# A two-layer hybrid trunk on one core: the opening with one load queue, a split one-pass norm weight, Pool's low parts and earlier squares

## Chip, cores and metric

The kernel runs on one core of a Trainium2 chip. The metric is device microseconds of one execution. All times in this document are microseconds unless marked otherwise.

## What is computed

The reference runs two layers over x, which is 256 tokens by 1024 features in float32. Each layer has a token mixer and a channel mixer, each of them between two RMS norms:

```python
for l in range(DEPTH):
    h = rms_norm(x, ln_mix_pre[l])
    x = x + rms_norm(hybrid_mixer(h, ...), ln_mix_post[l])
    h = rms_norm(x, ln_ffn_pre[l])
    x = x + rms_norm(conv_ffn(h, ...), ln_ffn_post[l])
```

The mixer projects h by one matrix w_in whose columns feed three head groups: MoBA attention with a relative bias from a table (rel_bias), latent attention with a low-rank query and key/value (each with an RMS norm of its own, q_norm and kv_norm, here called the norms of the latents), and forgetting attention. Their outputs are mixed by w_o. The channel mixer is a GeGLU network with a causal convolution of width 3.

## The kernel before

The two token tiles of 128 rows stand with tokens on partitions (`xt[0]`, `xt[1]`). A product is done in float32r, at one pass each, with both operands split into a high part (rounded to float32r) and a low part (what is left): three products, high·high, high·low and low·high, take the place of one of full precision.

Weights come in slabs of up to 128x1024 float32. The list of slabs is written down once, in order of use (`plan`): for the first layer four slabs "c" (latents, 128x832), four "v" (128x768), then qa0 and qa1 (128x1024), uq, uk, and so on. A slab is loaded into one of five staging buffers (`fetch`, line 195). Its high part is then rounded on ScalarE (`hi_next`, line 207) and its low part subtracted on VectorE (`lo_next`, line 214); the second of these frees the staging buffer, and the next slab's load can be issued. `slab` runs six slabs ahead of use, unless `hold` is set. High and low parts have eight buffers.

Each engine works through its own instructions in the order in which the program issues them. SyncE issues most loads, ScalarE and Pool (GpSimd) a few. In the opening of the first layer this order is written by hand:

- The prenorm of a tile (`prenorm`, line 287) takes two squares with accumulated sums on ScalarE (line 270), three small Pool steps that make the inverse root (lines 275 to 277), and two scalings on VectorE (line 291). They multiply x by the root and by the norm weight, which for the first layer stands in two PSUM banks: it has been spread over the partitions by products of a matrix `ones` with `g0`, whose first row is the weight (line 134).
- `to_feat` transposes a tile on TensorE (line 298) and splits it: high part on ScalarE (line 254), low part on VectorE (line 255). They go to `xh` and `xl`.
- `c_piece(t, h)` multiplies tile t by slab "c" h (lines 248, 249, 251), `v_piece` by slab "v" h. After the "c" pieces, `c_norm` does the norms of the latents: square on ScalarE (line 405), root on Pool (259, 260), scaling on VectorE (407), four times in turn. `c_feat` transposes their result (line 415) behind the "v" pieces, and then come the products with qa0, qa1 and the rest.
- The bias table is built by a small product (`bias_start`, line 329), copied to `rr`, written to memory (`sd`, line 334) and gathered back from there as `hk`, 128x6x256 (line 338), through Pool's queue. It is used much later, in `bias_end` (line 344).

In ScalarE's order the high parts of qa0 and qa1 stand ahead of the squares of the norms of the latents, in both kernels.

Of the kernel before, what the change touches and what calls it, by code (L numbers as in the profile page):

```python
# [10 lines left out]
F32 = mybir.dt.float32  # L11
F32R = mybir.dt.float32r
AF = mybir.ActivationFunctionType
ALU = mybir.AluOpType
AX = mybir.AxisListType

D = 1024
# [16 lines left out]
C_U, C_M, C_R = 0, 128, 384  # L34
# [30 lines left out]
def kernel(ctx: ExitStack, tc: tile.TileContext, x, rel_bias, ln_mix_pre, ln_mix_post,  # L65
                             ln_ffn_pre, ln_ffn_post, w_in, b_f, q_norm, kv_norm, w_uq, w_ukv, w_o,
                             w_up, conv_w, conv_b, w_down, cst_d, oh_d, out):
    nc = tc.nc
# [6 lines left out]
    lay = pool("lay", 1)  # L75
    work = pool("work", 2)
# [7 lines left out]
    def acc():  # L84
        return [wk(), wk()]
# [7 lines left out]
    def tok(t):  # L93
        return slice(t * 128, t * 128 + 128)
# [11 lines left out]


    ctx.enter_context(tc.manual_schedule())
    g0 = work.tile([128, D], F32, name="g0", tag="scr", bufs=2)
    nc.gpsimd.memset(g0, 0.0)  # L110
    oh = work.tile([32, 256 + HA], F32, name="oh", tag="pr", bufs=4)
    for c in (slice(0, 512), slice(512, 1024)):
        nc.sync.dma_start(xt[0][:, c], x_v[0][:, c])
    nc.scalar.dma_start(ident, cst_d[:, 0:128])
    nc.scalar.dma_start(g0[0:1, :], ln_mix_pre[0:1])
    ones = work.tile([128, 128], F32, name="ones", tag="pr", bufs=4)
    nc.vector.memset(ones, 0.0)
    nc.vector.memset(ones[0:1, :], 1.0)
    warm = t2([128, 512])
    nc.vector.memset(warm, 0.0)  # L120
    mhalf = const.tile([128, 1], F32, name="mhalf")
    nc.vector.memset(mhalf, -0.5)
    epsb = const.tile([128, 1], F32, name="epsb")
# [5 lines left out]
    mask = cst[:, C_M:C_M + 256]  # L129
    wps = wk()  # L130
    nc.tensor.matmul(wps, ones, warm, start=True, stop=True)
    gps0 = acc()
    for i in range(2):
        nc.tensor.matmul(gps0[i], ones, g0[:, 512 * i:512 * i + 512], start=True, stop=True)


    def plan():
# [70 lines left out]
        lows.append((h, lo, st, n))  # L208
        loaded[key] = (shaped(h, shp), shaped(lo, shp))

    def lo_next():
        if lows:
            h, lo, st, n = lows.pop(0)
            nc.vector.tensor_tensor(lo[:, :n], st[:, :n], h[:, :n].bitcast(F32), op=ALU.subtract)  # L214

    def split_next():
        hi_next()
        lo_next()
# [23 lines left out]
        nc.tensor.matmul(o, stat[0], mov[1], start=False, stop=False)  # L242
        nc.tensor.matmul(o, stat[1], mov[0], start=False, stop=stop)  # L243

    def mm3s(o, pairs, start, stop):
        n = len(pairs)
        for i, (stat, mov) in enumerate(pairs):
            nc.tensor.matmul(o, stat[0], mov[0], start=start and i == 0, stop=False)  # L248
            nc.tensor.matmul(o, stat[0], mov[1], start=False, stop=False)  # L249
        for i, (stat, mov) in enumerate(pairs):  # L250
            nc.tensor.matmul(o, stat[1], mov[0], start=False, stop=stop and i == n - 1)  # L251
# [13 lines left out]
    def rstd2(src, then=None):  # L265
        junk = work.tile([128, 512], mybir.dt.bfloat16, name="junk", bufs=1)
        ms = small.tile([128, 2], F32, name="ms")
        r = small.tile([128, 2], F32, name="r")
        for i in range(2):
            nc.scalar.activation(junk, src[i], AF.Square, scale=1.0 / 32, accum_out=ms[:, i:i + 1])  # L270
            if i == 0 and then is not None:
                then()

        def fin():
            nc.gpsimd.tensor_tensor(r[:, 0:1], ms[:, 0:1], epsb, op=ALU.add)
            nc.gpsimd.tensor_tensor(r[:, 1:2], r[:, 0:1], ms[:, 1:2], op=ALU.add)
            nc.gpsimd.tensor_tensor(r[:, 0:1], r[:, 1:2], mhalf, op=ALU.pow)
            return r[:, 0:1]
        return fin
# [1 line left out]
    def scr():  # L281
        return work.tile([128, D], F32, name="scr", bufs=2)

    def prenorm(t, g, then=None, mid=None):
        fin = rstd2([xt[t][:, c] for c in HALF], then)
        if mid is not None:
            mid()
        r = fin()
        hn = scr()
        for i in range(2):  # L290
            nc.vector.scalar_tensor_tensor(hn[:, HALF[i]], xt[t][:, HALF[i]], r, g[i], op0=ALU.mult, op1=ALU.mult)
        return hn

    def to_feat(t, hn, xh, xl):
        for q in range(2):
            ps = wk().rearrange("p (c f) -> p c f", c=4)
            for c in range(4):
                nc.tensor.transpose(ps[:, c, :], hn[:, (4 * q + c) * 128:(4 * q + c + 1) * 128], ident)  # L298
            s = (slice(None), slice(4 * q, 4 * q + 4), tok(t))
            split(ps, xh[s], xl[s])  # L300

# [17 lines left out]
    wbias = const.tile([128, HA, S], F32, name="wbias")  # L319

    hk = []

    def bias_loads():
        nc.gpsimd.dma_start(oh[:, :256], oh_d)
        nc.gpsimd.dma_start(oh[:, 256:], rel_bias)

    def bias_start():
        ps = wk()
# [25 lines left out]
    for l in range(L):  # L354
# [16 lines left out]
        def feat(i):  # L371
            return qs[i // 4][:, i % 4, :]

        def nat_piece(ps, nm, t, n, h):
            wh, wl = slab((l, nm, h))
            mm3s(ps[:, :n], [((xh[:, 2 * h + k, tok(t)], xl[:, 2 * h + k, tok(t)]), (wh[:, k, :], wl[:, k, :]))
                             for k in range(2)], h == 0, h == 3)

        def nat(nm, t, n):
            ps = wk()  # L380
# [208 lines left out]
        if l == 0:  # L589
            act_set(EXP_SET)  # L590
            fetch(1)
            hn = [prenorm(0, gps0, lambda: [nc.scalar.dma_start(xt[1][:, c], x_v[1][:, c]) for c in HALF]), None]
            fetch(2, nc.scalar)
            split_next()
            fetch(4, nc.scalar)
            to_feat(0, hn[0], xh, xl)
        else:
            hn = hn_next
# [1 line left out]
        vps = [wk(), wk()]  # L600

        def c_piece(t, h):
            nat_piece(cps[t], "c", t, 416, h)

        def v_piece(t, h):
            nat_piece(vps[t], "v", t, 384, h)
# [3 lines left out]

        if l == 0:
            hold[0] = True
            c_piece(0, 0)
            split_next()
            c_piece(0, 1)
            hn[1] = prenorm(1, gps0)
            split_next()
            bias_loads()
            to_feat(1, hn[1], xh, xl)
            small_loads()  # L620
            nc.sync.dma_start(cst[:, C_R:], cst_d[:, 256 + C_R:])
            hold[0] = False
            for t, h in ((1, 0), (1, 1), (0, 2), (1, 2), (0, 3), (1, 3)):
                c_piece(t, h)
            nc.vector.tensor_copy(identr, ident[:6, :6])
            cn = [c_norm(t, cps[t]) for t in range(2)]
            bias_start()
            for h in range(4):
                for t in range(2):
                    v_piece(t, h)  # L630
            nc.sync.dma_start(cst[:, :C_R], cst_d[:, 256:256 + C_R])
            v_end(0)
            v_end(1)
            c_feat(0, cn[0])
            c_feat(1, cn[1])
        else:
            small_loads()
            hold[0] = False
            c_piece(0, 0)
            c_piece(0, 1)  # L640
            c_piece(0, 2)
            c_piece(0, 3)
            cn0 = c_norm(0, cps[0])
            for h in range(3):
                v_piece(0, h)
            to_feat(1, hn[1], xh, xl)
            v_piece(0, 3)
            v_end(0)
            for h in range(4):
                c_piece(1, h)  # L650
            cn1 = c_norm(1, cps[1])
            c_feat(0, cn0)
            for h in range(4):
                v_piece(1, h)
            v_end(1)
            c_feat(1, cn1)
# [306 lines left out]
```

## Time and profile before

| | |
|---|---|
| runs shown | 654.88, 649.19, 650.67; median 650.67 |
| profiled execution, its own time | 651.27 |
| its span in the trace | 649.5 |
| granted TensorE clock, mean | 0.994 |
| TensorE busy | 631.4 us, 97% of the span |
| VectorE, ScalarE, Pool busy | 452.4, 381.2, 31.6 us |
| loaded from memory | 107.78 MB |

The span runs from the first to the last instruction; the execution's own time has 1.8 us around it. Durations come from the one profiled execution. Engines are called PE (TensorE), DVE (VectorE), ACT (ScalarE), POOL and SP; PEld is TensorE's weight load. In a timeline a row starts with its start and duration; "x4" means four instructions merged, and a bracket holds the idle time before them and what ended it. Matmuls are pipelined, so a duration is longer than the distance to the next one.

### The profile page before, as it was taken

The page shows a single profiled execution, that of the slowest core. Times are in us where ns is not written, and L with a number is a line of the kernel's source. Part 1 is how long each engine was busy: PE and PEld are TensorE (multiplying, and loading weights), DVE is VectorE, ACT ScalarE, POOL GpSimd, SP SyncE. Part 2 cuts the span into 40 slices and gives each one's busy share as a digit, 9 for nine tenths or more (in the row PEclk, how much of TensorE's full clock was granted, in tenths as well). Part 3 has the DMA queues.
Part 4 walks back from the last instruction along what each step waited for, and adds up shares of the span by engine and source line. Part 5 has one row for each costly group of instructions (what it writes and reads, how often), then busy time and mean ns, then how long its engine had stood idle before and what let it go on. Part 6 is the DMA issues. An engine that isn't in the chain of part 4 may idle for free.

```text
span 649.5 us, 11307 instructions
## 1 busy us (share of the span) xinstructions
PE 631.4 (97%) x4290; PEld 569.7 (88%) x4290; DVE 452.4 (70%) x891; ACT 381.2 (59%) x729; POOL 31.6 (5%) x74
## 2 busy tenths in 40 slices
PE   7999999999999999999899999999999999999996
PEld 3998987799999999999688988878998999999974
DVE  4674786576878777766676567757587887777663
ACT  4577557656656555545556666566575665555541
POOL 2110000110000000000031000002100000000001
PEclk9999999999999999999899999999999999999998
DMA  7876343356356765553545833334554665556401
GB/s 248 246 246 211 130 161 100 98 169 193 132 173 217 263 224 170 187 181 107 153 126 150 290 131 132 129 98 129 175 170 149 229 227 195 195 195 195 161 2 65
DMA packets 79402, 109.57 MB, mean 169 GB/s; under 512 B 4013, under 2 KB 69267, under 8 KB 79348
## 3 DMA queue, kind: packets, MB, share of 16 engines
q1 hardware_dynamic: 77762, 106.09, 49.8%
q10 hardware_dynamic: 1250, 1.87, 0.8%
q0 software_dynamic: 336, 0.90, 0.4%
q8 instruction: 33, 0.54, 0.3%
q14 instruction: 21, 0.17, 0.1%
HBM read 107.78 MB, written 1.06 MB: 168 GB/s over the span
## 4 chain that ended last, share of the span: by engine, by line
PE 84%; DVE 6%; ACT 3%; DMA 3%; issue 2%; POOL 1%; DVEq 0%; POOLq 0%; ACTq 0%; SPq 0%
PE wk L248 17%; PE wk L249 16%; PE wk L251 16%; PE wk L241 8%; PE wk L242 8%; PE wk L243 8%; DVE wl L214 2%; DMA st<-in_w_in_dram 2%; PE wk L557 2%; PE wk L565 2%; PE wk L524 1%; ACT wh L207 1%; PE wk L522 1%; ACT junk L270 1%; PE wk L298 1%
## 5 line engine op out<-in xcount | busy, mean ns | idle before, releaser
L214 DVE TENSOR_TENSOR wl<-st,wh 128x1024 fp32r<-128x1024 f32 (+3 forms) x200 | 229.4, 1183 | 80.8 <-ACT wh L207 79.8
L207 ACT ACTIVATE wh<-st 128x1024 fp32r<-128x1024 f32 (+3 forms) x200 | 195.8, 1021 | 39.3 <-PE wk L249 13.7
L248 PE MATMUL wk<-xh,wh 128*128 128x256 f32 x768 | 194.3, 285 | 0.1
L249 PE MATMUL wk<-xl,wh 128*128 128x256 f32 x768 | 192.4, 283 | 0.0
L248 PEld LDWEIGHTS wk<-xh,wh 128*128 128x128 f32 x768 | 147.0, 191 | 2.8 <-issue 1.3
L249 PEld LDWEIGHTS wk<-xl,wh 128*128 128x128 f32 x768 | 147.2, 192 | 0.7
L251 PE MATMUL wk<-xh,wl 128*128 128x256 f32 x768 | 123.6, 283 | 0.1
L251 PEld LDWEIGHTS wk<-xh,wl 128*128 128x128 f32 x768 | 105.9, 192 | 0.5 <-DVE wl L214 0.5
L242 PE MATMUL wk<-wl,hp 128*128 128x512 f32 x176 | 70.0, 398 | 2.0 <-DVE wl L214 2.0
L241 PE MATMUL wk<-wh,hp 128*128 128x512 f32 x176 | 69.6, 396 | 0.8 <-ACT wh L207 0.8
L243 PE MATMUL wk<-wh,hp 128*128 128x512 f32 x176 | 69.1, 393 | 0.0
L249 PE MATMUL wk<-wl,xh 128*128 128x256 f32 (+3 forms) x224 | 65.6, 312 | 2.9 <-DVE wl L214 2.9
L248 PE MATMUL wk<-wh,xh 128*128 128x256 f32 (+3 forms) x224 | 66.8, 316 | 1.2 <-ACT xh L254 0.6
L837 ACT ACTIVATE t<-wk,cv 128x256 f32<-128x256 f32 x88 | 43.7, 559 | 40.8 <-PE wk L251 40.7
L845 DVE SCALAR_TENSOR_TENSOR t<-wk,cv,t 128x255 f32<-128x255 f32 x88 | 41.9, 476 | 32.1 <-ACT t L837 32.1
L251 PE MATMUL wk<-wh,xl 128*128 128x256 f32 (+3 forms) x224 | 45.9, 309 | 0.9 <-DVE xl L255 0.9
L249 PEld LDWEIGHTS wk<-wl,xh 128*128 128x128 f32 x224 | 42.6, 190 | 4.7 <-DVE wl L214 4.5
L248 PEld LDWEIGHTS wk<-wh,xh 128*128 128x128 f32 x224 | 42.7, 191 | 3.1 <-ACT wh L207 1.3
L847 DVE SCALAR_TENSOR_TENSOR t<-wk,cv,t 128x254 f32<-128x254 f32 x88 | 42.4, 482 | 3.1
L242 PEld LDWEIGHTS wk<-wl,hp 128*128 128x128 f32 x176 | 33.5, 190 | 10.5 <-DVE wl L214 4.3
L241 PEld LDWEIGHTS wk<-wh,hp 128*128 128x128 f32 x176 | 33.4, 190 | 7.7 <-ACT wh L207 1.2
L243 PEld LDWEIGHTS wk<-wh,hp 128*128 128x128 f32 x176 | 33.5, 190 | 6.9
(149 smaller groups left out, 688.5 us busy)
## 6 DMA issues: line engine op xcount, KB each, us to landing
st<-in_w_up_dram SPq DMA_DIRECT2D x88, 512.0 KB, 4.7
st<-in_w_down_dram SPq DMA_DIRECT2D x44, 512.0 KB, 4.6
st<-in_w_in_dram SPq DMA_DIRECT2D x24, 512.0 KB, 4.8
st<-in_w_o_dram SPq DMA_DIRECT2D x16, 512.0 KB, 3.1
st<-in_w_in_dram SPq DMA_DIRECT2D x8, 390.0 KB, 7.1
st<-in_w_in_dram SPq DMA_DIRECT2D x8, 384.0 KB, 3.1
st<-in_w_in_dram SPq DMA_DIRECT2D x5, 416.0 KB, 3.3
st<-in_w_in_dram ACTq DMA_DIRECT2D x3, 416.0 KB, 6.5
```

The lines of the kernel that those rows point to most:

```text
L207: nc.scalar.activation(h[:, :n], st[:, :n], AF.Copy)
L214: nc.vector.tensor_tensor(lo[:, :n], st[:, :n], h[:, :n].bitcast(F32), op=ALU.subtract)
L241: nc.tensor.matmul(o, stat[0], mov[0], start=start, stop=False)
L242: nc.tensor.matmul(o, stat[0], mov[1], start=False, stop=False)
L243: nc.tensor.matmul(o, stat[1], mov[0], start=False, stop=stop)
L248: nc.tensor.matmul(o, stat[0], mov[0], start=start and i == 0, stop=False)
L249: nc.tensor.matmul(o, stat[0], mov[1], start=False, stop=False)
L251: nc.tensor.matmul(o, stat[1], mov[0], start=False, stop=stop and i == n - 1)
L557: nc.tensor.transpose(pT[:, kb * 128:kb * 128 + 128], pr[:, kb * 128:kb * 128 + 128], ident)
L837: nc.scalar.activation(y[:, g, :], us[a][:, g, :], AF.Identity, scale=cv[:, 88 + cj:89 + cj], bias=cv[:, 132 + cj:133 + cj])
L845: nc.vector.scalar_tensor_tensor(y[:, g, 1:], u[:, g, :S - 1], cv[:, 44 + cj:45 + cj], y[:, g, 1:], op0=ALU.mult, op1=ALU.add)
L847: nc.vector.scalar_tensor_tensor(y[:, g, 2:], u[:, g, :S - 2], cv[:, cj:cj + 1], y[:, g, 2:], op0=ALU.mult, op1=ALU.add)
```

## The change

The change rewrites the opening of the first layer. All big loads go through SyncE's queue in this order: x of tile 0, slab c0, x of tile 1, c1, c2, c3, v0, then the small tables of the norms, then the rest; only the norm weight's row and the identity stay with ScalarE, and the two loads for the bias table go to Pool at the very start. The norm weight is split into a high and a low row and spread by two one-pass products for each half, on full `ones`. The low parts of c0 and c1 are subtracted on Pool. The squares of tile 1 stand ahead of the split of tile 0 on ScalarE. The bias product comes before the transposes of tile 1. The "c" pieces of the first layer are multiplied in another order (`late`): the products that need a slab's low part come last.

```diff
-    g0 = work.tile([128, D], F32, name="g0", tag="scr", bufs=2)
-    nc.gpsimd.memset(g0, 0.0)
+    g0 = work.tile([1, D], F32, name="g0", tag="scr", bufs=2)
+    nc.scalar.dma_start(g0, ln_mix_pre[0:1])
...
+    gh = lay.tile([128, D], F32R, name="gain", bufs=2)
+    gl = lay.tile([128, D], F32R, name="gain", bufs=2)
+    nc.gpsimd.memset(gh.bitcast(F32), 0.0)
+    nc.gpsimd.memset(gl.bitcast(F32), 0.0)
+    nc.gpsimd.dma_start(oh[:, :256], oh_d)
+    nc.gpsimd.dma_start(oh[:, 256:], rel_bias)
...
-    nc.scalar.dma_start(g0[0:1, :], ln_mix_pre[0:1])
...
-    nc.vector.memset(ones, 0.0)
-    nc.vector.memset(ones[0:1, :], 1.0)
+    nc.vector.memset(ones, 1.0)
...
+    oner = work.tile([128, 128], F32R, name="oner", tag="pr", bufs=4)
+    nc.vector.tensor_copy(oner, ones)
...
+    nc.tensor.matmul(wps[:, :256], ones, warm[:, :256], start=True, stop=True)
...
     for i in range(2):
-        nc.tensor.matmul(gps0[i], ones, g0[:, 512 * i:512 * i + 512], start=True, stop=True)
+        c = slice(512 * i, 512 * i + 512)
+        nc.vector.tensor_copy(gh[0:1, c], g0[:, c])
+        nc.vector.tensor_tensor(gl[0:1, c], g0[:, c], gh[0:1, c].bitcast(F32), op=ALU.subtract)
+        nc.tensor.matmul(gps0[i], oner, gh[:, c], start=True, stop=False)
+        nc.tensor.matmul(gps0[i], oner, gl[:, c], start=False, stop=True)
...
-    def lo_next():
+    def lo_next(eng=None):
...
-            nc.vector.tensor_tensor(lo[:, :n], st[:, :n], h[:, :n].bitcast(F32), op=ALU.subtract)
+            (eng or nc.vector).tensor_tensor(lo[:, :n], st[:, :n], h[:, :n].bitcast(F32), op=ALU.subtract)
...
+        if late:
+            for i, (stat, mov) in enumerate(pairs):
+                nc.tensor.matmul(o, stat[0], mov[0], start=start and i == 0, stop=False)
+            for i, (stat, mov) in enumerate(pairs):
+                nc.tensor.matmul(o, stat[1], mov[0], start=False, stop=False)
+            for i, (stat, mov) in enumerate(pairs):
+                nc.tensor.matmul(o, stat[0], mov[1], start=False, stop=stop and i == n - 1)
+            return
...
             fetch(1)
-            hn = [prenorm(0, gps0, lambda: [nc.scalar.dma_start(xt[1][:, c], x_v[1][:, c]) for c in HALF]), None]
-            fetch(2, nc.scalar)
-            split_next()
-            fetch(4, nc.scalar)
+            for c in HALF:
+                nc.sync.dma_start(xt[1][:, c], x_v[1][:, c])
+            fetch()
+            small_loads()
+            nc.sync.dma_start(cst[:, C_R:], cst_d[:, 256 + C_R:])
+            hn = [prenorm(0, gps0), None]
+            hi_next()
+            lo_next(nc.gpsimd)
+            fin1 = rstd2([xt[1][:, c] for c in HALF])
             to_feat(0, hn[0], xh, xl)
...
             hold[0] = True
+            fetch()
+            hn[1] = prenorm(1, gps0, fin=fin1)
             c_piece(0, 0)
-            split_next()
+            hi_next()
+            lo_next(nc.gpsimd)
             c_piece(0, 1)
-            hn[1] = prenorm(1, gps0)
-            split_next()
-            bias_loads()
-            to_feat(1, hn[1], xh, xl)
-            small_loads()
-            nc.sync.dma_start(cst[:, C_R:], cst_d[:, 256 + C_R:])
+            bias_start()
+            to_feat(1, hn[1], xh, xl, hi_next)
+            lo_next()
             hold[0] = False
...
             cn = [c_norm(t, cps[t]) for t in range(2)]
-            bias_start()
```

In VectorE's order before, from the scalings of tile 0 (`scr<-x_84`) on, the low parts of c0, c1 and c2 (`wl`, 128x832) stand between the steps of the two tiles; `xl` is the low part of a transposed tile and `x_85` is tile 1:

```order
L291 SCALAR_TENSOR_TENSOR scr<-x_84,r,wk 128x512 x2
L214 TENSOR_TENSOR wl<-st,wh 128x832
L255 TENSOR_TENSOR xl<-wk,xh 128x4x128 x2
L214 TENSOR_TENSOR wl<-st,wh 128x832
L291 SCALAR_TENSOR_TENSOR scr<-x_85,r,wk 128x512 x2
L214 TENSOR_TENSOR wl<-st,wh 128x832
L255 TENSOR_TENSOR xl<-wk,xh 128x4x128 x2
L214 TENSOR_TENSOR wl<-st,wh 128x832
L214 TENSOR_TENSOR wl<-st,wh 128x768 x4
```

The same place in the changed kernel, where `gain` is the split norm weight and `rr` the bias row:

```order
L144 TENSOR_TENSOR gain<-g_90,gain 1x512
L311 SCALAR_TENSOR_TENSOR scr<-x_84,r,wk 128x512 x2
L275 TENSOR_TENSOR xl<-wk,xh 128x4x128 x2
L311 SCALAR_TENSOR_TENSOR scr<-x_85,r,wk 128x512 x2
L349 MEMSET rr 6x128
L350 COPY rr<-wk 6x256
L275 TENSOR_TENSOR xl<-wk,xh 128x4x128 x2
L226 TENSOR_TENSOR wl<-st,wh 128x832 x2
L226 TENSOR_TENSOR wl<-st,wh 128x768 x4
```

The low parts of c0 and c1 have gone, that of c2 has moved from ahead of tile 1's `xl` to behind it, and the copy of the bias row has come in between.

In Pool's order before, the bias row is written out (`sd`) and gathered (`hk`) behind the four roots of the norms of the latents, of which the last is the first two rows here:

```order
L259 TENSOR_TENSOR r<-ms,epsb 128x1
L260 TENSOR_TENSOR r<-r,mhalf 128x1
L334 DMA sd<-rr 6x384
L336 DMA jm<-in_cst_dram 128x128
L338 DMA hk<-sd 128x6x256
L275 TENSOR_TENSOR r<-ms,epsb 128x1
```

In the changed kernel the same three DMAs follow the second low part, and the roots of the latents (L279) come behind them:

```order
L226 TENSOR_TENSOR wl<-st,wh 128x832
L295 TENSOR_TENSOR r<-ms,epsb 128x1
L296 TENSOR_TENSOR r<-r,ms 128x1
L297 TENSOR_TENSOR r<-r,mhalf 128x1
L226 TENSOR_TENSOR wl<-st,wh 128x832
L352 DMA sd<-rr 6x384
L354 DMA jm<-in_cst_dram 128x128
L356 DMA hk<-sd 128x6x256
L279 TENSOR_TENSOR r<-ms,epsb 128x1
```

The gather has moved past the roots of the latents, and the two low parts stand on either side of tile 1's root.

## Rows read from the trace of the kernel before

**Rows 1.** Stretches: length, busy PE PEld DVE ACT POOL, PEclk, DMA share, GB/s.
```profile
0.00:16.88 16.88, 12.13 (x34) 6.51 (x34) 7.73 (x15) 8.44 (x15) 4.39 (x13) 1.00 0.75 245
16.88:60.00 43.12, 43.03 (x284) 39.40 (x284) 28.56 (x67) 27.92 (x58) 5.62 (x11) 1.00 0.75 241
60.00:130.00 70.00, 69.91 (x471) 58.40 (x470) 47.01 (x154) 45.84 (x120) 2.91 (x6) 1.00 0.37 127
```

**Rows 2.** The chain that ended last, 0 to 34 us: start, duration, what.
```profile
4.93 6.52 DMA st<-in_w_in_dram
...
14.73 0.76 DVE scr L291
...
19.25 0.96 DVE wl L214
...
20.23 5.51 DMA st<-in_w_in_dram
...
25.84 1.06 ACT wh L207
...
33.73 0.33 PE wk L415
```

**Rows 3.** Timeline of the opening, all engines: norm weight, tile 0, products, bias product.
```profile
1.72 0.49 ACTq L115 DMA_DIRECT2D g<-in_ln_mix_pre_dram  x1
...
4.78 3.75 PE L134 MATMUL wk<-g,ones 128*128 128x512 f32 x4 [0.86 <-DMA g<-in_ln_mix_pre_dram]
4.89 0.63 ACT L270 ACTIVATE junk<-x 128x512 bf16<-128x512 f32 x1 [0.23 <-ACT junk L270]
...
5.68 0.90 ACT L207 ACTIVATE wh<-st 128x832 fp32r<-128x832 f32 x1
...
6.02 0.55 POOL L277 TENSOR_TENSOR r<-r,mhalf 128x1 f32<-128x1 f32 x1
...
8.57 0.75 DVE L291 SCALAR_TENSOR_TENSOR scr<-x,r,wk 128x512 f32<-128x512 f32 x1 [0.89 <-PE wk L134]
...
10.14 0.69 PE L248 MATMUL wk<-wh,xh 128*128 128x416 f32 x1
...
10.63 0.47 PE L249 MATMUL wk<-wl,xh 128*128 128x416 f32 x1
...
18.97 0.54 PE L251 MATMUL wk<-wh,xl 128*128 128x416 f32 x2
...
23.98 0.59 PE L329 MATMUL wk<-oh 32*6 32x256 f32 x2
```

**Rows 4.** The same timeline: Pool's small steps and DVE work beside them.
```profile
0.24 0.10 POOL L947 MEMSET const-float32-0.0<- 128x1 f32 x1 [0.24 <-issue]
...
0.74 0.95 POOL L110 MEMSET g<- 128x1024 f32 x1 [0.29 <-POOLq L947]
...
4.74 0.19 POOL L275 TENSOR_TENSOR r<-ms,epsb 128x1 f32<-128x1 f32 x1 [3.05 <-ACT junk L270]
...
10.17 0.68 DVE L255 TENSOR_TENSOR xl<-wk,xh 128x512 fp32r<-128x512 f32 x1
...
26.93 1.23 DVE L214 TENSOR_TENSOR wl<-st,wh 128x1024 fp32r<-128x1024 f32 x1 [1.38 <-ACT wh L207]
...
27.34 0.86 POOL L259 TENSOR_TENSOR r<-ms,epsb 128x1 f32<-128x1 f32 x1 [11.50 <-ACT t L405]
```

**Rows 5.** The gather: its issue; DMA totals of 41 to 45 us, by queue.
```profile
37.15 0.86 POOL L338 DMA_DIRECT2D hk<-sd  x1 [1.07 <-DMA sd<-rr]
...
DMA packets 580, 1.35 MB, mean 336 GB/s; under 512 B 34, under 2 KB 387, under 8 KB 579
...
q0 software_dynamic: 207, 0.79, 59.9%
q1 hardware_dynamic: 372, 0.55, 39.5%
...
st<-in_w_in_dram SPq DMA_DIRECT2D x2, 512.0 KB, 7.9
```

More of the change, by code (lines that the diff above doesn't have):

```diff
@@ L243, in mm3, with mm3s @@
         nc.tensor.matmul(o, stat[1], mov[0], start=False, stop=stop)
-    def mm3s(o, pairs, start, stop):
+    def mm3s(o, pairs, start, stop, late=False):
         n = len(pairs)
+        if late:
[6 more added lines that the diff above has]
+            return
         for i, (stat, mov) in enumerate(pairs):
@@ L282, in scr, with prenorm @@
         return work.tile([128, D], F32, name="scr", bufs=2)
-    def prenorm(t, g, then=None, mid=None):
-        fin = rstd2([xt[t][:, c] for c in HALF], then)
+    def prenorm(t, g, then=None, mid=None, fin=None):
+        fin = fin or rstd2([xt[t][:, c] for c in HALF], then)
         if mid is not None:
@@ L292, in prenorm, with to_feat @@
         return hn
-    def to_feat(t, hn, xh, xl):
+    def to_feat(t, hn, xh, xl, mid=None):
         for q in range(2):
@@ L298, in to_feat @@
                 nc.tensor.transpose(ps[:, c, :], hn[:, (4 * q + c) * 128:(4 * q + c + 1) * 128], ident)
+            if q == 0 and mid is not None:
+                mid()
             s = (slice(None), slice(4 * q, 4 * q + 4), tok(t))
@@ L321 @@
     hk = []
-    def bias_loads():
-        nc.gpsimd.dma_start(oh[:, :256], oh_d)
-        nc.gpsimd.dma_start(oh[:, 256:], rel_bias)
     def bias_start():
@@ L372, in feat, with nat_piece @@
             return qs[i // 4][:, i % 4, :]
-        def nat_piece(ps, nm, t, n, h):
+        def nat_piece(ps, nm, t, n, h, late=False):
             wh, wl = slab((l, nm, h))
             mm3s(ps[:, :n], [((xh[:, 2 * h + k, tok(t)], xl[:, 2 * h + k, tok(t)]), (wh[:, k, :], wl[:, k, :]))
-                             for k in range(2)], h == 0, h == 3)
+                             for k in range(2)], h == 0, h == 3, late)
         def nat(nm, t, n):
@@ L602, in c_piece @@
         def c_piece(t, h):
-            nat_piece(cps[t], "c", t, 416, h)
+            nat_piece(cps[t], "c", t, 416, h, l == 0)
         def v_piece(t, h):
```

## The prediction

> **What bounds the kernel now.** I read the busy time by stretch first, because the change touches only the first 35 us. TensorE (PE) is busy 12.13 of the first 16.88 us, then 43.03 of the next 43.12 and 69.91 of the 70 after that [rows 1]; the first stretch ends where the first product of tile 1 starts. So the matmuls set the time from 16.88 us on, and only the 4.75 us that PE idles before that, and the slowness of its work there, are open to this change. Whatever moves the point from which PE runs without a wait moves the end by as much.
>
> The second view, the chain that ended last, says what sets that point, and the reader should follow it by its gaps [rows 2]. It isn't PE at 16.88. The chain runs over slab c1 of the weights (issued 4.93, 6.52 us to land), the prenorm of tile 1 (14.73), its transposes and its split, the low part of slab v0 on VectorE (19.25 to 20.21), and then leaves the engines: the end of that subtraction frees a staging buffer, SyncE issues slab qa1 at 20.23, and qa1 lands 5.51 us later. Its high part (ACT, 25.84) stands ahead of the latent norms on ScalarE, these are a serial chain of ACT, Pool and DVE steps, and the last transposes that need them start at 33.73. Only from there on does nothing but PE stand in the chain. So this is the point to move: PE waits for slab qa1 by way of the norms.
>
> Third, the timeline of the opening gives the prices [rows 3]. [...]
>
> **The change part by part, up to slab qa1.** *The norm weight.* The row is issued at 0.74 instead of 1.72 [rows 3]; it was there at about 4.7, so now at 3.7. DVE then does four one-partition passes of 512 columns; the nearest row is the 512-column subtraction at 0.68 [rows 4], and with 0.6 each they end at 6.1. The four full-precision products took 3.75 us, that is 0.94 each [rows 3] and two passes in each; a one-pass product costs about half, and the last one ends near 6.7 instead of 8.5. ScalarE no longer issues loads between the two squares, so the second one starts some 0.2 us before 4.89, and the inverse root, which ended at 6.57, ends at 6.35. The two scalings stand at 6.4 and 7.1 (the second was at 8.57 [rows 3]), the transposes start near 7.2, the split at 8.35 and the first product of slab c0 at 9.0 (10.14 [rows 3]). The added 256-column warm-up product ends at about 4.2, before the row's high part is there, so it costs nothing. Pool's second memset and its two loads for the bias, moved ahead of the root, take 0.95 and 1.2 us and end at 3.9, while the root begins at 4.7.
>
> *Loads.* With everything on SyncE's queue in order of need, tile 1 of x and c1 come right behind c0, which ACT rounds from 5.68 on [rows 3]: 0.94 MB more at the 336 GB/s of a full stretch [rows 5] puts c1 at about 8.5 instead of 11.45. ScalarE gets to it at 9.8, behind the split, so the load is no longer what is late; the high part ends at 10.7.
>
> *Low parts on Pool.* The trace of before has no such subtraction. The lower bound is Pool's memset, 0.95 us for 1024 columns [rows 4], so 0.77 for 832. The upper one is three such streams, two in and one out: 2.3. The ratio of a one-column add to a one-column memset, 0.19 to 0.10 [rows 4], would give 1.5. I take 1.9, between that and the upper end. The first subtraction lies beside the transposes and costs nothing. The second starts at 10.7 and ends at 12.6, and the last two products of c1 for tile 0, ahead of everything of tile 1 in PE's order, wait for it. [...]
>
> Pool can also be held up. At 27.34 an add of one column took 0.86 us instead of 0.19 while a DVE subtraction of 1.23 us ran [rows 4]. Read plainly, any DVE work beside it blocks Pool: the second subtraction would then wait for the scalings of tile 1, which end at 11.85, and everything behind would be 1.15 us later. [...]
>
> *Tile 1.* Its squares come at 6.5 to 8.0 and its scalings at 10.45 to 11.85, behind tile 0's low parts on DVE. Then PE: two products to 13.0, the bias product (0.59 us at 23.98 [rows 3], now out of the later stream) to 13.5, eight transposes, split at 14.15, and the first product of tile 1 at 14.8 where it was at 16.88: 2.1 us sooner. [...] With the Pool bounds the 14.8 is 13.7 to 15.2.
>
> *What is late next.* In DVE's new order the low parts of c2, c3 and v0 all come behind the split of tile 1, whereas c2's was ahead of it. The split ends at 16.1, three subtractions of 0.95 end at 18.95, and qa1 is issued at 19.0 instead of 20.23. Of the 2.1 us, 1.2 are left here. Two added waits are covered. DVE's copy of the bias row waits for the bias product (13.5); behind it stands the split of tile 1, which comes at 14.8 anyway. In the late order the third product of tile 1 already needs the low part of x and waits some 0.35 us, which vanishes in PE's wait for the norms. The small loads of the norms, moved ahead on SyncE, stand between v0 and v1, whose staging buffers come free later still.
>
> *The bias gather.* This is what I think decides. The gather of the bias table, 768 KB through Pool's queue, was issued at 37.15 [rows 5], when the norms were over. Now it follows the second Pool subtraction: the bias row is copied at about 13.9, written out by 15.9 and the gather issued at 16.2. Its data flowed in 41 to 45 us, four to eight us behind its issue; now that is 20 to 24, where qa0 and qa1 have to move. In 41 to 45 it moved 0.79 MB and the weights only 0.55 [rows 5], at 336 GB/s in all: the weights lose up to 2.35 us. Two weight slabs in flight in that stretch took 7.9 us to land [rows 5], where qa1 took 5.51 without the gather [rows 2]. So qa1 takes 5.5 to 7.9 us; I take 6.7, the middle, since the gather's start can miss qa0 and part of what qa1 took was queueing behind slabs that now come a little earlier. That is 19.0 + 6.7 = 25.7, against 25.74.
>
> **Sum.** PE's own stream would be 2.1 + 0.6 = 2.7 us ahead. The norms begin 0.1 us earlier, so PE stands still for 2.6 us before the transposes of the norms, and the end moves by −0.1. The profiled execution took 651.27 (span 649.5 and 1.8 around it), so 651.2; it lies 0.6 above the median of the runs shown, 650.67, on which I put the difference: 650.6. The rest of the program is the same in both, and PE hardly waits in it up to 130 us [rows 1], so a shift at 33.73 reaches the end.
>
> **Rivals.** *The gather misses qa1 (faster).* If its data come before or behind, or the engines serve the weights first, qa1 lands in 5.5 us or less: 24.5 or sooner, and the gain is 1.2 to 2.7, where PE's own stream caps it. That gives 648.0 to 649.4, centre 648.7. For it: the gather's data started nearly four us after its issue, and a delay of a few us is all it needs. Against: 0.79 MB in four us is most of what the engines moved.
>
> *The gather takes its full price (slower).* At 7.9 us qa1 lands at 26.9, the norms start 1.1 us later than before, and PE waits for them: 651.8, and 652.5 where the low clock level also holds. It decides from a landing time of 6.8 us on. For it: 7.9 is a measured time in that company. Against: in 41 to 45 us more slabs were queued ahead than there will be.
>
> *The lead never comes about.* If a Pool subtraction takes 4 us or more, tile 1 starts where it did, the gather still moves along, and qa1 lands at 27.8: 652.7. Nothing in the rows puts Pool that high.
>
> **How the numbers follow.** Forecast (lead eaten, within 1 us of 650.6) 0.45; gather misses 0.30; full price 0.20; no lead 0.05. The range must hold 648.0 and 652.7 with the runs' own spread of a few tenths of a per cent, so 647.4 to 653.2. About 1% (6.5 us) is what a measurement of this kernel can tell from no change. All of PE's idle time in the opening is 4.75 us, so none of the cases is faster by that, nor slower: 0.02 for faster, 0.95 within, 0.03 for slower, for what I have not thought of.
>
> **What would show it.** Right: the first product of tile 1 near 14.8, qa1 issued near 19.0 and landing near 25.7 with the gather's bytes in 20 to 24, and two to three us of PE idle just before the six transposes of the norms. Wrong: no PE idle there and qa1 landed by 24 (gather missed), Pool subtractions far from 1.9, products still 0.35 apart after 14.8, or a new wait of PE behind 34 us.

## The result: slower by 0.7%

The changed kernel took 655.84 (median of 14 runs, 653.66 to 658.26), the kernel before 651.78 beside it (14 runs). The ratio is 1.0066, with a 95% interval of 1.0050 to 1.0082. Forecast was 650.6 with a range up to 653.2: the time lies outside it, while the step is still under the 1% that the chances were about. The profiled execution took 656.73, its span is 654.7, which is 5.2 over the span of before. The medians are 4.1 apart, and the forecast stood on three runs of the kernel before with a median of 650.67; the rows below account for the 5.2 of the two profiled executions.

**Where it went.** The stretches of [rows 1], in the changed kernel, and behind them two of 5 us (columns as there):

```profile
0.00:16.88 16.88, 12.66 (x41) 8.21 (x42) 9.28 (x20) 9.13 (x17) 10.43 (x18) 0.90 0.81 257
16.88:60.00 43.12, 39.22 (x238) 35.62 (x237) 24.70 (x56) 23.45 (x49) 4.47 (x9) 0.92 0.75 233
60.00:130.00 70.00, 69.91 (x492) 59.18 (x491) 45.96 (x156) 45.02 (x121) 0.00 (x0) 1.00 0.37 121
30.00:35.00 5.00, 2.52 (x13) 1.67 (x11) 2.67 (x10) 1.37 (x7) 2.87 (x6) 0.91 0.79 221
35.00:40.00 5.00, 3.58 (x16) 3.18 (x17) 3.64 (x10) 4.59 (x10) 0.74 (x2) 0.50 0.10 14
```

From 60 us on PE is as busy as before (69.91 of 70). In 16.88 to 60 it idles 3.90 us where it idled 0.09, and the granted clock of that stretch is 0.92. Both come from 30 to 41 us: PE stands still for nearly four us there, and afterwards works at a granted clock of 0.50 in 35 to 40, below called the lower level; the upper one is the 1.00 of 60 to 130.

**The chain** that ended last has the links of [rows 2] from the low part of slab v0 (18.96) on, and one of them is much longer. Ahead of that it now runs over slab c0, where it ran over c1:

```profile
1.66 5.35 DMA st<-in_w_in_dram
...
9.30 0.49 ACT xh L274
...
18.96 0.96 DVE wl L226
19.94 9.18 DMA st<-in_w_in_dram
29.22 1.06 ACT wh L219
```

Slab qa1 is issued at 19.94, 0.29 sooner than before, and takes 9.18 us to land instead of 5.51. Its high part starts at 29.22 instead of 25.84, the serial chain of the norms follows, and the last transpose that needs them stands at 37.11. On PE's own timeline one sees the waits, and behind them the products of qa group 0 (those with qa0 and qa1), at first 0.21 us apart from start to start:

```profile
32.80 0.44 PE L433 MATMUL wk<-ident,t 128*128 128x128 f32 x2 [1.19 <-DVE t L425]
34.48 0.48 PE L433 MATMUL wk<-ident,t 128*128 128x128 f32 x1 [1.24 <-DVE t L425]
35.43 0.69 PE L433 MATMUL wk<-ident,t 128*128 128x128 f32 x2 [0.47 <-DVE t L425]
37.11 0.47 PE L433 MATMUL wk<-ident,t 128*128 128x128 f32 x1 [0.99 <-DVE t L425]
37.24 0.56 PE L268 MATMUL wk<-xh,wh 128*128 128x256 f32 x1
...
40.37 0.42 PE L268 MATMUL wk<-xh,wh 128*128 128x256 f32 x1
40.58 0.42 PE L269 MATMUL wk<-xl,wh 128*128 128x256 f32 x1
...
44.70 0.34 PE L253 MATMUL wk<-wh,cT 128*128 128x384 f32 x1
```

The last row, the first product of the latents' up-projection, is a good mark, since it ends the products of qa group 0. It stands at 44.70. In before the group starts at 33.81, goes 0.12 apart, and the mark is the last of these rows:

```profile
33.81 0.36 PE L248 MATMUL wk<-xh,wh 128*128 128x256 f32 x1
...
35.33 0.28 PE L248 MATMUL wk<-xh,wh 128*128 128x256 f32 x1
35.45 0.28 PE L249 MATMUL wk<-xl,wh 128*128 128x256 f32 x1
...
39.65 0.34 PE L241 MATMUL wk<-wh,cT 128*128 128x384 f32 x1
```

So the loss up to there is 5.05 us. The group itself took 7.46 us (37.24 to 44.70) where it took 5.84 (33.81 to 39.65): 1.62 us are the lower clock (0.50 granted in 37.24 to 40.50, where before shows 1.00 over its whole group), and the other 3.4 are qa1's later landing (29.22 against 25.84, 3.38).

**The opening**, as in [rows 3] and [rows 4]:

```profile
5.60 0.63 PE L146 MATMUL wk<-gain,oner 128*128 128x512 f32 x1
...
7.04 0.90 ACT L219 ACTIVATE wh<-st 128x832 fp32r<-128x832 f32 x1 [1.18 <-DMA st<-in_w_in_dram]
...
7.67 1.32 PE L318 MATMUL wk<-ident,scr 128*128 128x128 f32 x8 [1.44 <-DVE scr L311]
...
8.01 1.94 POOL L226 TENSOR_TENSOR wl<-st,wh 128x832 fp32r<-128x832 f32 x1 [1.18 <-ACT wh L219]
...
9.84 0.76 PE L261 MATMUL wk<-wh,xh 128*128 128x416 f32 x2 [0.85 <-ACT xh L274]
...
11.14 1.97 POOL L226 TENSOR_TENSOR wl<-st,wh 128x832 fp32r<-128x832 f32 x1
...
12.12 0.90 PE L261 MATMUL wk<-wh,xh 128*128 128x416 f32 x2
12.81 0.90 PE L263 MATMUL wk<-wh,xl 128*128 128x416 f32 x2
...
14.04 0.59 PE L347 MATMUL wk<-oh 32*6 32x256 f32 x2
...
15.91 0.64 PE L261 MATMUL wk<-wh,xh 128*128 128x416 f32 x2 [0.25 <-ACT xh L274]
```

The one-pass products of the norm weight end at 6.23, the high part of c0 waits for its load and starts at 7.04 (5.68 in [rows 3]), Pool's subtractions take 1.94 and 1.97, the bias product stands at 14.04, and the first product of tile 1 at 15.91, 0.97 sooner than before and not 2.1.

**The gather.** Pool issues it at 17.57, behind the write of the bias row. Behind that row stand the DMA totals of 21 to 23 us, by queue (packets, MB, share of 16 engines), which show who moved what:

```profile
17.57 0.86 POOL L356 DMA_DIRECT2D hk<-sd  x1 [1.01 <-DMA sd<-rr]
...
DMA packets 187, 0.53 MB, mean 264 GB/s; under 512 B 0, under 2 KB 93, under 8 KB 187
...
q0 software_dynamic: 94, 0.39, 70.8%
q1 hardware_dynamic: 93, 0.14, 24.8%
```

q0 is Pool's queue, q1 the weights'. They moved the same number of packets, but a packet of the gather held 4.1 KB (0.39 MB by 94) and one of the weights 1.5 KB.

### The profile page after: what moved, and what is told of

The parts are those of the page before. It is cut to its first block, busy times and chain, and to the rows that moved or that the text cites. A ratio compares the mean times of both kernels' runs of the same rounds, so it can differ in the third digit from the quotient of the medians.

```text
span 654.7 us, 11317 instructions
## 1 busy us (share of the span) xinstructions
PE 633.1 (97%) x4292; PEld 572.9 (88%) x4292; DVE 453.7 (69%) x893; ACT 380.9 (58%) x729; POOL 36.6 (6%) x77
## 4 chain that ended last, share of the span: by engine, by line
PE 85%; DVE 5%; DMA 3%; ACT 3%; issue 2%; POOL 1%; SPq 0%; DVEq 0%; POOLq 0%; ACTq 0%
PE wk L268 17%; PE wk L269 17%; PE wk L271 17%; PE wk L253 8%; PE wk L254 8%; PE wk L255 8%; DMA st<-in_w_in_dram 2%; DVE wl L226 2%; PE wk L575 2%; PE wk L583 2%; PE wk L542 1%; PE wk L540 1%; ACT junk L290 1%; ACT wh L219 1%; PE wk L318 1%
## 5 line engine op out<-in xcount | busy, mean ns | idle before, releaser
L269 PE MATMUL wk<-wl,xh 128*128 128x256 f32 (+3 forms) x208 | 60.3, 310 | 2.4 <-DVE wl L226 2.4
L268 PE MATMUL wk<-wh,xh 128*128 128x256 f32 (+3 forms) x208 | 61.1, 314 | 0.9 <-ACT xh L274 0.9
L269 PEld LDWEIGHTS wk<-wl,xh 128*128 128x128 f32 x208 | 40.0, 192 | 3.9 <-DVE wl L226 3.7
L271 PE MATMUL wk<-wh,xl 128*128 128x256 f32 (+3 forms) x208 | 42.2, 310 | 0.9 <-DVE xl L275 0.9
L268 PEld LDWEIGHTS wk<-wh,xh 128*128 128x128 f32 x208 | 40.0, 192 | 1.7 <-ACT xh L274 1.2
L295 POOL TENSOR_TENSOR r<-ms,epsb 128x1 f32<-128x1 f32 x16 | 8.3, 520 | 571.2 <-ACT junk L290 571.2
L253 PEld LDWEIGHTS wk<-wh,hp 128*128 128x128 f32 x176 | 33.1, 188 | 7.6 <-ACT wh L219 1.2
```

The source lines that it names most:

```text
L253: nc.tensor.matmul(o, stat[0], mov[0], start=start, stop=False)
```

## The experiments

All times are ratios to the kernel before on the same chip. Single profiles of the changed opening differ in one thing that doesn't go with the edits: the high part of slab c0 starts anywhere from 6.4 to 8.1 us, and the opening moves with it (in the changed kernel's profile c0 is at 7.04 and the first product of tile 1 at 15.91; in experiments 5, 6 and 9 at 8.0 to 8.1 and 18.0 to 18.1). So profiles are compared from one instruction to the next rather than by clock time, and the verdicts go by the ratios.

**1. The gather back behind the norms.** Edit to the changed kernel; all three loads on Pool's queue (the bias row's write, jm, the gather) move:

```diff
+        hk.append(rr)
+
+    def bias_gather():
+        rr = hk.pop()
         sd = drm.tile([HA, 384], F32, name="sd")
         nc.gpsimd.dma_start(sd, rr)
...
             cn = [c_norm(t, cps[t]) for t in range(2)]
+            bias_gather()
```

> The changed kernel with one part undone: the writing-out and the gather of the bias row go back behind the roots of the latent norms, the bias product and its copy stay early. Theory G (the gather beside qa1 is to blame): qa1 lands at about 24 instead of 29.1 us, PE waits less than 1 us before the transposes of the norms, its clock stays at the upper level there, and the end comes 5 us sooner than in the changed kernel, 1 us sooner than before: ratio to before 0.998. Rival O (the opening itself, its queue order and the lower clock level until 13.6 us): nothing is gained, ratio 1.006.

Ratio 0.9991 (0.9972 to 1.0010). From the chain and PE's timeline in its profile:

```profile
25.16 1.06 ACT wh L219
...
33.06 0.33 PE L437 MATMUL wk<-ident,t 128*128 128x128 f32 x1 [1.12 <-DVE t L429]
...
38.97 0.34 PE L253 MATMUL wk<-wh,cT 128*128 128x384 f32 x1
```

qa1, issued at 19.72, is rounded at 25.16, so it took at most 5.4 us. PE waits 1.1 us before one transpose, stays at the upper level (1.00 granted in 30 to 45, qa group 0 in 5.82 us), and the mark of the up-projection stands at 38.97, 0.68 before its place in before, which is just by how much qa1's rounding came sooner (25.16 against 25.84). The early loads are the whole loss (experiment 9 tells the large one from the two small ones). Without them what is left of the change can't be told from none: by the ratio 0.6 us less, with an interval from 1.8 less to 0.7 more.

**2. The early gather alone, in the kernel before.** There `bias_loads()` went to the start and `bias_start()` ahead of tile 1's transposes.

> The kernel before with that one part of the change alone: the two bias loads at the start, and bias product, copy, writing-out and gather ahead of the transposes of tile 1. Theory G: the gather is issued near 20 us, qa1 takes 8 to 9 us to land instead of 5.5, PE waits 3 us or more for the norms and falls to the lower clock level; 3 to 5 us slower than before, ratio 1.005 to 1.008. Rival O: within 0.5 us of before, ratio 1.000.

Ratio 0.9993 (0.9974 to 1.0011): the expectation missed, and usefully. The write of the bias row waited, and the gather was issued at 20.73, right before qa1:

```profile
20.73 0.86 POOL L338 DMA_DIRECT2D hk<-sd  x1 [1.92 <-DMA sd<-rr]
```

From 14 to 24 us its queue moved 0.07 MB, which is jm and the bias row; of the gather's 0.79 MB nothing had moved. qa1, issued at 20.91, was rounded at 25.86, as in before. So the early gather as such doesn't cost; its time against qa1 does. The issue is three us later than in the changed kernel, and the data start five us later (24 instead of 19). This is the first rival of the prediction, seen alive.

**3. PE kept busy in the wait.** Unread 128-column full-precision products (6, 6, 2 and 5, so 19 and not the 16 of the expectation) between the transposes of the norms in the changed kernel.

> The changed kernel with products nobody reads (16 of 128 columns, on the identity) put into the gaps between the transposes of the latent norms, some 3 us of work at the lower and 3.3 at full precision in all. If part of the loss is the lower clock level after PE's wait (products 0.21 apart instead of 0.12 for 3.4 us), the level stays up and the end comes 1 to 2 us sooner than in the changed kernel: ratio to before 1.004. If the level is set by something else: ratio 1.006 to 1.007.

Ratio 1.0097 (1.0073 to 1.0120). The clock did stay up (1.00 granted in 31 to 45): the products of qa group 0 ran 0.12 apart and the group took 5.83 us, as in before.

```profile
38.21 1.35 PE L433 MATMUL wk<-ident 128*128 128x128 f32 x10 [0.54 <-DVE rp L414]
...
39.43 0.36 PE L268 MATMUL wk<-xh,wh 128*128 128x256 f32 x1
...
45.26 0.34 PE L253 MATMUL wk<-wh,cT 128*128 128x384 f32 x1
```

But the last five products (ten instructions in the row) stood in front of the last transpose, whose input was ready at 37.8, and held it up to 39.4. So this shows the price of the clock (7.46 against 5.83 for the same group), and isn't a cure.

**4. The products of qa1 first.** In the changed kernel the products of qa group 0 go ahead of the norm transposes, to fill the wait.

> The changed kernel with the products of the first qa group (5.8 us of PE work that need only qa0, qa1 and x) put between the last v piece and the transposes of the norms, one half ahead of each tile's. The gather stays early. Theory G says PE's wait is for the norms alone, so this work fills it: 4 to 6 us sooner than the changed kernel, ratio to before 0.998 to 1.000, qa1 still landing at 28 to 29. If PE waits for qa1's weights as such, the wait only moves ahead of that group: ratio 1.003 or more.

Ratio 1.0071 (1.0046 to 1.0097), a miss: neither of the two cases. The wait before the transposes went, and stood one step later, at the up-projection, which waits for the split of the latents behind other low parts on DVE:

```profile
40.06 0.44 PE L253 MATMUL wk<-wh,cT 128*128 128x384 f32 x1 [1.42 <-ACT cT L274]
...
41.82 0.44 PE L255 MATMUL wk<-wh,cT 128*128 128x384 f32 x1 [1.15 <-DVE cT L275]
```

**5. A plain load in the gather's place.** Experiment 1 and, at the early place, a load of the same size from other addresses:

```diff
+        src = w_up[0]
+        nc.gpsimd.dma_start(hk[0], bass.AP(tensor=src.tensor, offset=src.offset, ap=[[2 * FF, 128], [512, HA], [1, S]]))
```

> Edit: the bias gather goes back behind the norm roots, as in the first experiment, and in its early place a plain load of the same 768 KB, in 1 KB pieces from different addresses of another weight, goes through Pool's queue into the same tile (it is overwritten by the real gather later; nothing reads it). Two theories of why the gather holds qa1 up. Bytes: what counts is 768 KB more beside the weights. Then qa1 takes about as long to land as in the changed kernel, 8 to 9.2 us, and the time is 1.004 to 1.007 of before. Pattern: the gather reads one region of 9 KB over and over, and the DMA engines moved only about 255 GB/s in all while its data flowed, against 336 in a full stretch without it. Then the plain load takes its share at full rate, qa1 lands 1 to 2 us sooner than the 29.1 of the changed kernel, and the time is 1.000 to 1.003.

Ratio 1.0012 (0.9983 to 1.0041). That tells nothing on the question: with no write to wait for, the load was issued at 14.69 and had moved before qa1 was issued (22.38), which then took 5.87 us. It repeats the lesson of experiment 2 from the other side.

**6. The norms ahead of qa1's high part on ScalarE**, the gather still early:

```diff
+            ahead[0] = 4
...
-            cn = [c_norm(t, cps[t]) for t in range(2)]
+            cn = [c_norm(0, cps[0])]
+            convert(8)
+            cn.append(c_norm(1, cps[1]))
+            ahead[0] = AHEAD
```

> Edit to the changed kernel: on ScalarE the squares, roots and scalings of the latents' norms stand ahead of the high part of qa1 (they need slabs v3 and before it only), so that the norms no longer wait for qa1; the gather stays early. Theory 1, the late landing of qa1 costs time only through ScalarE's order (high part of qa1, then norms, then PE's transposes): the norms then start when slab v3's products are done, PE's wait before the norm transposes shrinks from 4 us to 2 or less, and the time is 1.000 to 1.003 of before. Theory 2, the weights as a whole come too late for PE's products while the gather takes the DMA engines (qa2, qa3, uq too): PE's wait moves to the products of qa1 and the time stays at 1.004 to 1.007.

Ratio 1.0008 (0.9983 to 1.0032), by theory 1. The six transposes follow the last product of v3 with no wait:

```profile
34.01 0.51 PE L272 MATMUL wk<-wh,xl 128*128 128x384 f32 x2
34.36 1.04 PE L434 MATMUL wk<-ident,t 128*128 128x128 f32 x6
```

By the ratios, then, a late qa1 costs most of its time through ScalarE's order: 1.0008 instead of 1.0066 with the gather still early. The rows alone are weaker evidence, since c0 was late in this execution and the products of v3 ended at 34.4, where in the changed kernel's profile they end at 31.6.

**7. Both: gather late, norms first.**

> Edit: both of it, the gather back behind the norm roots and the norms ahead of the high part of qa1. If qa1 is the last thing between the lead of the opening (about 1.2 us, first product of tile 1 at 15.7 instead of 16.88) and the rest, PE then waits for nothing before the norm transposes and the first product of the head stage comes 1.5 to 2 us sooner than in before: ratio 0.997. If the next wait (the norm chain itself, or slab qa1 at its own products) stands close behind, 0.999 to 1.000.

Ratio 0.9979 (0.9958 to 1.0001), so a gain is likely but not shown by the ratio. In its profile PE never idles from 16.88 to 60, and the mark stands at 37.66, 1.99 before its place in before:

```profile
16.88:60.00 43.12, 43.12 (x296) 40.21 (x295) 28.98 (x71) 27.79 (x60) 5.41 (x11) 1.00 0.78 249
...
37.66 0.34 PE L254 MATMUL wk<-wh,cT 128*128 128x384 f32 x1
```

**8. The norms first in the kernel before.**

> Edit to the kernel before: only the norms ahead of the high part of qa1. PE waits little before the norm transposes there (its products of v3 end about when the norms do), so at most 0.4 us can be won: ratio 0.999 to 1.000. If it gives as much as the same order does on top of the late gather, the change's opening adds nothing to it.

Ratio 1.0018 (0.9995 to 1.0042), no gain; a loss can't be told from none. That fits an order that pays only where PE's stream is ahead of the norms; experiment 6 shows that it pays beside the early gather, and beside the late one (7 against 1) the intervals overlap.

**9. The plain load at the gather's own time.** The bias rows lie in the gather's target buffer, so that the plain load of experiment 5 has to wait for the write of the bias row; the gather itself is late.

> Edit to the changed kernel: the rows that the gather would spread are kept in its target buffer, the gather itself goes back behind the norm roots, and in its place on Pool's queue, waiting for the write of the bias row just as the gather did (so issued at 17 to 18 with the opening of the changed kernel), a plain load of the same 768 KB in 1 KB pieces from addresses that do not overlap. Nothing reads what it brings. This repeats experiment 5 at the gather's own time. Theory bytes: the weights lose to 768 KB whatever is read. qa1 then takes 8 to 9.2 us to land, ratio 1.004 to 1.007. Theory pattern: the gather costs so much because it reads 9 KB over and over (some 255 GB/s in all in its stretch instead of 336 or more). Then the plain load moves at the full rate and qa1 lands 1 to 2 us sooner than 29.1, 7 to 8 us after its issue; ratio 1.000 to 1.003.

Ratio 1.0058 (1.0036 to 1.0081), as theory bytes had it. The plain load was issued at 19.16, and its bytes moved in 21 to 23.5:

```profile
DMA packets 244, 0.81 MB, mean 323 GB/s; under 512 B 15, under 2 KB 66, under 8 KB 244
...
q0 software_dynamic: 193, 0.73, 81.8%
q1 hardware_dynamic: 51, 0.08, 20.6%
...
22.41 7.01 DMA st<-in_w_in_dram
```

The last row is of its chain: qa1 took 7.01. The nearest profile without the load in flight is experiment 5's, with c0 as late and qa1 issued at 22.38: there qa1 took 5.87, its high part started 1.17 sooner, and the mark of the up-projection stood at 42.15 instead of 44.81. The other 1.4 of these 2.7 us are the clock: qa group 0 took 5.82 there and 7.26 here, at a granted clock of 1.00 there and 0.74 here in 35 to 40.

By the time, theory bytes holds: the ratio lies within the interval of the changed kernel's, so bytes suffice for the loss. By the landing, theory pattern's 7 to 8 us came true, but the rates don't show a pattern. In 21 to 23 Pool's queue had the engines nearly to itself (SyncE's moved 3 packets), so the 323 GB/s can't be set against the 264 beside the gather; over the whole flight of qa1 the engines moved 317 GB/s here and 314 in the changed kernel. Only 0.25 MB of the plain load moved after qa1's issue, 0.65 of the gather.

**10 to 12. The rest of the opening**, on top of experiment 7. Experiment 10 fills PE's gap of 2.2 us before the first transposes with unread products on zeros; 12 keeps back the two products that need Pool's second subtraction until tile 1's transposes are issued; 11 does both:

```diff
+    wps = wk()
+    nc.tensor.matmul(wps[:, :512], ones, warm[:, :512], start=True, stop=True)
+    nc.tensor.matmul(wps[:, :256], ones, warm[:, :256], start=True, stop=True)
...
-            c_piece(0, 1)
+            rest = []
+            c_piece(0, 1, rest)
             bias_start()
             to_feat(1, hn[1], xh, xl, hi_next)
+            rest.pop()()
```

> Edit to experiment 7 (gather late, norms ahead of qa1's high part): 768 columns of unread full-precision products on zeros behind the four products of the norm weight, where PE is idle for 2.2 us before the first transposes (5.79 to 7.98). Theory: the lower clock level lasts to 13.5 in the changed kernel because its short products leave that gap; the kernel before had its long products there and the level rose at 10.9. With the gap filled it rises at 11 to 12. But the last two products of slab c1 for tile 0 wait for Pool's second subtraction, which ends at 13.2, so the products before them only get a longer wait: first product of tile 1 at 15.4 to 15.7, ratio 0.997 to 0.998, as experiment 7. Rival: the gap has nothing to do with the level, products stay 0.35 apart to 13.5.

Ratio 0.9972 (0.9950 to 0.9994). The products of c0 are 0.19 apart from 10.7 on (1.00 granted in 10 to 15, 0.80 in experiment 7), PE then waits 0.83 for Pool (was 0.46), as expected, and tile 1 starts at 15.27.

> Edit to experiment 10: also the last two products of slab c1 for tile 0 (those that need Pool's subtraction) go behind the bias product and the transposes of tile 1 in PE's order. If Pool's subtraction and the clock level are the two things that hold the opening, the first product of tile 1 starts at 14.2 to 14.6 and, since nothing else was waited for in experiment 7 up to the head stage, the whole gain is kept: 1 to 1.5 us below experiment 7, ratio 0.995 to 0.996. Rival: tile 1's squares and scalings, or the weights (slab qa1 and those behind it), are next, and it stays at 0.997 to 0.998.

Ratio 0.9948 (0.9929 to 0.9966), 647.66 against 650.74: the best version, and faster than the kernel before beyond its interval. Its timeline, which has the later landing of c0, still brings tile 1 at 15.13:

```profile
14.64 0.63 PE L271 MATMUL wk<-wl,xh 128*128 128x416 f32 x2
15.13 0.65 PE L265 MATMUL wk<-wh,xh 128*128 128x416 f32 x2
```

The two kept-back products now fill the wait for tile 1's split.

> Edit to experiment 7: only the last two products of slab c1 for tile 0 behind tile 1's transposes, no filled gap. The wait for Pool there was 0.46 us in experiment 7; the products before it run at the lower level. First product of tile 1 at 15.2 to 15.4, ratio 0.997. If it does as well as experiment 11, the clock level of the opening costs nothing.

Ratio 0.9976 (0.9957 to 0.9995), as expected, but the first product of tile 1 came at 17.28 and not at 15.2 to 15.4. Its median is 1.7 us above experiment 11's on the same chip (649.32 against 647.66), the intervals overlap, and in its profile, where c0 is late too (7.58, 8.04 in experiment 11's), products are 0.35 apart until 18 us (0.66 granted in 10 to 15, 0.65 in 15 to 20). So the clock of the opening seems worth some 1.5 us; that is read from two medians and not certain.

## Why the prediction was wrong

**Right.** The frame: PE's stream is bounded from 16.88 on, qa1 by way of the norms is the point that counts, the early gather collides with qa1, and "PE stands still for 2.6 us before the transposes of the norms" (it came as 3.9 in four pieces). Experiment 1 shows that this collision is all of the loss. Pool's subtraction was taken at 1.9 and took 1.94 and 1.97. The second one ran from 11.14 to 13.11 beside the scalings of tile 1 on DVE (11.04 to 12.45) and was not held up: it took 0.03 more than the first, beside which DVE was idle from 8.28 to 9.82. So the plain reading of [rows 4] was wrong; that its 1.15 us stayed out of the sum was the author's estimate.

**The step that failed: "qa1 takes 5.5 to 7.9 us; I take 6.7, the middle, since the gather's start can miss qa0".** It took 9.18, past the upper bound too. The DMA totals from qa1's issue to its landing, in before (20.23 to 25.74), in experiment 1 (19.72 to 25.06 at the latest) and in the changed kernel (19.94 to 29.12, with its queues):

```profile
DMA packets 1451, 1.66 MB, mean 301 GB/s; under 512 B 56, under 2 KB 1349, under 8 KB 1451
...
DMA packets 1535, 1.76 MB, mean 330 GB/s; under 512 B 57, under 2 KB 1504, under 8 KB 1535
...
DMA packets 2047, 2.88 MB, mean 314 GB/s; under 512 B 94, under 2 KB 1768, under 8 KB 2046
...
q1 hardware_dynamic: 1872, 2.22, 73.4%
q0 software_dynamic: 174, 0.65, 25.0%
```

The engines were not slower over the flight than in before (314 against 301 GB/s); they had more to move. First, there is no half price: 0.65 of the gather's 0.79 MB moved in that time, at 314 GB/s 2.1 us, where the text had worked out 2.35 in full and then halved it. Second, 2.22 MB of weights moved where in before it was 1.66, which is 1.8 us more. Together with the 0.2 us that the higher rate gives back this is the difference of 3.7 (9.18 against 5.51). Against experiment 1 the extra weights are mostly slabs issued behind qa1: from v3's issue at 18.17, when SyncE's queue had nothing else in flight (no packet of it in 17 to 18), to qa1's landing it moved 2.22 MB, and v3, qa0 and qa1 are 1.44 of them. In experiment 1 the same count leaves 0.4 MB (1.85 from 17.95 to 25.06) instead of 0.8. Why later slabs got ahead of qa1's last bytes, and more of them beside the gather, no run shows. Nor does each byte in flight cost its full time everywhere: in experiment 2 0.37 MB of the gather moved in qa1's flight, and it took 4.9 us. The bound of 7.9 was one sample of a different mixture and no bound.

**The term that was left out: what the wait does to the clock.** I had not priced what follows the predicted wait before the norms at all. The wait came, and the granted clock of 35 to 40 was 0.50: 1.62 us for qa group 0. In experiment 1, where PE waits 1.1 us, the clock stayed at 1.00 and there was no such price. No run shows the 0.7 us that the 652.5 of a rival has for the low clock level; the runs showed these 1.62 us behind the wait, and for the opening some 1.5 by two medians (experiments 11 and 12). Against before the sum is 3.4 + 1.6 = 5.0, of 5.2 between the spans.

**The lead was mis-sized as well, and that counts.** qa1 was to be issued at 19.0 and came at 19.94; with the 2.5 us of its flight (9.18 for 6.7) and the 1.6 of the clock these 0.9 make up 5.0 of the 5.3 us by which the span (654.7) missed the one forecast (649.4, that of before less 0.1). Tile 1 was to start at 14.8 and came at 15.91. Of that, 0.84 stands ahead of the first product of c0 (9.84 for 9.0). The text let ACT round c0 from 5.68 on, as in before; it had to wait for the load until 7.04, and the squares of tile 1 (7.84 for 6.5) and the split of tile 0 (9.3 for 8.35) moved behind it. That is no accident of one execution: c0's high part starts at 6.4 to 8.1 in the eleven profiles with the changed opening, and at 5.7 to 6.2 in the three with the opening of before. Which part of the new order of loads makes c0 late was not tried. The rest is the clock: the products stayed 0.35 apart until 13.5 (0.50 granted in 10.9 to 13.5), where before they were 0.19 apart from 10.9 on (1.00 granted). The long full-precision products of the norm weight had kept PE working from 4.78 on, and the short ones leave a gap from 6.23 to 7.67. The low clock level was in the text, without a chance of its own. Experiment 10 shows that the gap matters: with it filled they are 0.19 apart from 10.7, in experiment 7, with c0 as early, from 12.3. A misreading had no consequence: the x4 of the norm weight's products are two products of two instructions each, not four products, and a one-pass product took about 0.43 from start to start where 0.47 was used, half of an instruction's 0.94 ([rows 3]).

**The rivals.** "The gather takes its full price" had the right mechanism and 0.20; its 651.8 was too low by four us: 0.9 from qa1's issue, 1.3 from its flight (9.18 for 7.9) and 1.6 from the clock. "The gather misses qa1" is what experiment 2 did in the kernel before.

## What to carry to other kernels

Before moving a large load forward, list what else will be in flight in its new place and charge its full bytes, not half of them, to the last transfer of that batch that something waits for. What is issued behind that transfer isn't free either: here 0.4 to 0.8 MB of it had moved before qa1 landed. When an order of loads is rewritten, ask of each load, also the one that comes first, whether it still lands when it did. A wait on TensorE can be priced twice, by its length and by the products that follow at the lower clock (1.6 us behind waits of 3.9 in all, nothing behind one of 1.1), and short products in place of long ones can keep the clock down in a stretch that looked idle anyway (0.50 granted in 10.9 to 13.5 here, 1.00 in 10 to 15 with the gap filled in experiment 10). When one slab sets the pace by way of an in-order engine, look whether the work behind it needs that slab at all: putting the norms ahead of qa1's high part took the ratio from 1.0066 to 1.0008 with the gather still early.

## What was not expected of the hardware

In 20 to 23 us of the changed kernel both queues had work and moved packets one for one (94 and 93 in 21 to 23), so that the weights, with 1.5 KB in a packet, got a quarter of the bytes beside the gather's 4.1 KB. It isn't one for one in every stretch: in 22 to 23 us of experiment 9, with v3 issued at 20.64, Pool's queue moved 92 packets and SyncE's 3. The sizes could have been read from the row of before (207 packets with 0.79 MB, 372 with 0.55 [rows 5]).
